# Written order for operand sums and early output splits, and one more step in two streams of a hybrid decoder layer

## The chip, the cores and the metric

One core of a Trainium2 chip runs the whole layer. The metric is the time of one execution on the device in microseconds, the median of three runs. TensorE (PE) multiplies matrices, and its weight loads are shown apart as PEld; VectorE (DVE) and ScalarE (ACT) do element-wise work; GpSimd (POOL) and SyncE (SP) mostly issue transfers here. PSUM is the memory that PE writes its sums to, in banks of 512 floats a partition.

## What is computed

For x of 2048 tokens by 1024 columns, in float32 throughout:

```python
h = _rmsnorm(x, norm1_w); proj = h @ w_in
o_hg = _hgrn2_mixer(...)   # 4 heads of 128: q, f, i, g; gated recurrence, then
#   o = o * lax.rsqrt(mean(o * o, axis=-1) + NORM_EPS) * norm_w * silu(g)
o_rw = _rwkv7_mixer(...)   # 8 heads of 64: S = S*w + (S a) b^T + v k^T, y = S r; group norm, gate
x = x + concat([o_hg, o_rw]) @ w_out
x = x + _conv_ffn(_rmsnorm(x, norm2_w), w_up, conv_w, conv_b, w_down)   # 1024 -> 5632 -> 2816 -> 1024
return _rmsnorm(x, final_norm_w)
```

## The kernel before

**Dense products.** Every large product keeps float32 accuracy by three matmuls in a reduced format: each operand is split into a rounded high part and the rest (`split`, L250 to L256, and `split_to`, L246 to L248: a copy on ACT, then a subtraction on DVE), and `mm3` (L268 to L272) issues high x high, high x low and low x high. The FFN products use a scheme with sums of operand blocks; `four_sums` (L238 to L244) makes four such sums on DVE.

**Two stages.** Stage one (`phase1`) covers the projections, both recurrences and three of the four output projections; stage two the last output projection and the FFN. Stage one walks over 4 blocks of 512 tokens. Three Python generators write its work down in turns:

- `dense`: jobs of 24 dense matmuls for 128 columns of the input projection (tile `pj`, two PSUM banks by turns, evacuated to `hf`, `hv`, `sgm`, `rkv` and others by `act` at L122 and by DVE), and in between the output projections (`out_block`), transposes (`turn`) and some set-up for stage two.
- `rw_stream`: eight calls of `rw_super`, two per block, each four RWKV heads: preparation, a small triangular solve on DVE (L793 to L814), the solve's matmuls (L821, L834, L847), copies of their result by ACT into `UV` and `M`, then state products (L867, L881, L895) and the state recurrence (L905 to L912).
- `hg_stream`: sixteen calls of `hg_unit`, one HGRN head each; at its end the output sums (L1064, L1065), their square, the split of the square (`osq` to `part`), two matmuls with a matrix of ones (L1083, L1084) for the mean square, Ln and Exp on ACT, and two products on DVE.

The driver takes one step (up to the next `yield`) of `rw_stream`, one of `hg_stream`, and then dense work worth 2000 ns by its own estimate (`TICK`).

**Set-up inside stage one.** `sum_load` (L459) loads four 128 x 1024 pieces of the normalised activations `h2d` into one row tile `xt`; `sum_make` calls `four_sums` on them and stores the results to `Ts`; both run twice (m = 0, 1), in the last block. `o_take` (L474) loads, four times, a piece of the mixer output of block 2 as `oraw` and splits it into `ohl`, which takes the place of the row tile; `out_block(2)` uses it as its first operand.

**What sets the order.** The kernel is written for a tile framework. [...] `tc.keep_in_program_order(i)` forbids the scheduler to put instruction i ahead of the one that was written just before it on the same engine. Functions of ACT come in tables; `act` (L111) ties an activation to the load of its table in written order, and a load is inserted where the next function in written order is in another table.

Of the kernel before, what the change touches and what calls it, by code (L numbers as in the profile page):

```python
# [67 lines left out]
def tile_layer(ctx, tc, consts, x, norm1_w, w_in, hg_lb_logits, hg_norm_w, rw_shift_mu, rw_w0, rw_w2,  # L68
# [4 lines left out]
    V, S, TE = nc.vector, nc.scalar, nc.tensor  # L73
# [40 lines left out]
    def act(out_, in_, func, **kw):  # L114

        want = tables.get(func)
        if want is not None and want != tab["now"]:
            pre = S.preload_act_table_set(want)
            for u_ in tab["uses"]:
                tc.add_manual_dep(pre.ins, u_.ins.name, NOSYNC, reason="table order")  # L120
            tab.update(now=want, pre=pre, uses=[])
        i_ = S.activation(out_, in_, func, **kw)  # L122
        if want is not None:
            tc.add_manual_dep(i_.ins, tab["pre"].ins.name, NOSYNC, reason="table order")
            tab["uses"].append(i_)
        return i_
# [13 lines left out]
    with tc.tile_pool(name="vp", bufs=1, reuse_waits="tile") as vp, tc.tile_pool(name="ps0", bufs=1, space=PSUM, reuse_waits="tile") as pools["ps"]:  # L140
        rows = vp.tile([P, P], F32, name="rows")
# [95 lines left out]

    def four_sums(b11, b12, b21, b22):  # L238

        V.tensor_sub(b11, b12, b11)  # L240
        V.tensor_sub(b12, b22, b12)
        V.tensor_sub(b22, b22, b11)
        V.tensor_sub(b21, b21, b22)
        return b11, b22, b12, b21  # L244

    def split_to(hi, lo, src):  # L246
        c_ = S.copy(hi, src)
        return c_, V.tensor_sub(lo, src, hi.bitcast(F32))  # L248
# [25 lines left out]
    def phase1(c1):  # L274
# [22 lines left out]
        def bank(kind):  # L297
            return ps.tile([P, 512], F32, tag=kind, name=kind, bufs=2)
# [119 lines left out]
        rows = {}  # L418
# [49 lines left out]
        def sum_make(m):  # L468
            def f():
                for i, t_ in enumerate(four_sums(*rows.pop(("S", m)))):  # L470
                    dma(tdst(0, i, 2 * m, 2), t_)
            return f

        def o_take(m):  # L474

            def f():
                if m == 0:
                    t_ = xp_.tile([P, 2, 2, 4, 256], F32R, tag="xt", name="ohl", bufs=1)
                    rows["O"] = [[t_[:, c, i] for i in range(2)] for c in range(2)]
                t_ = wp.tile([P, 2, 256], F32, tag="wraw", name="oraw", bufs=4)  # L480
                dma(t_, oT[2][2 * m * P:2 * (m + 1) * P, 0:256].rearrange("(k p) t -> p k t", p=P))
                ks = slice(2 * (m % 2), 2 * (m % 2) + 2)
                split_to(rows["O"][0][m // 2][:, ks, :], rows["O"][1][m // 2][:, ks, :], t_)
            return f

        def to_h(k, tp, w):
# [160 lines left out]
        def rw_super(nb, s_):  # L647
# [6 lines left out]
            def tile_(tag, shape, name):  # L654
                return rp.tile([P] + shape, F32, tag=tag, name=name)

            def bank2():
                return ps.tile([P, 2, BLK], F32, tag="rw", name="rw", bufs=2)

            def parts(src):  # L660
                hi, lo = (rp.tile([P, 2, BLK], F32R, tag=tag, name="part") for tag in ("XH", "E"))
                split_to(hi, lo, src)
                return hi, lo
# [134 lines left out]
            for j in range(31):  # L798
# [6 lines left out]
                if j % 4 == 3:  # L805
                    yield
            TZ = tile_("XH", [16, 16, 2], "TZ")
            V.transpose(TZ.rearrange("p c m f -> p (c m f)"), Ti.rearrange("m t c -> m c t"))
# [47 lines left out]
            for e in range(2):  # L856
                r0, c0 = er0(e), col0(1, e)
                act(M[r0:r0 + 64, 0, 1, :, :, 0:64], quv[1][c0:c0 + 64, :, :, 0:64], AF.Copy)
            yield
            XH = tile_("XH", [2, 9, 64], "XH")  # L860
            V.tensor_copy(XH[:, :, 0, :], Xc[:, 2 * s_:2 * s_ + 2, :])
            xp = bank2()
# [36 lines left out]
            for ch in range(8):  # L899
                b, e = ch // 2, ch % 2  # L900
                cs_ = slice(ch * 64, ch * 64 + 64)
                for u in U:
                    for h in range(2):
                        hr = slice(h * 64, h * 64 + 64)
                        TE.matmul(xp[hr, u, cs_], M[hr, 1, u, b, e, 0:64], XH[hr, u, ch, :], start=False,  # L905
                                  stop=ch == 7, tile_position=(h * 64, h * 64), skip_group_check=True)
                for u in U:
                    for h in range(2):
                        hr, c0 = slice(h * 64, h * 64 + 64), (h ^ u) * 64
                        TE.matmul(yp[c0:c0 + 64, u, cs_], XH[hr, u, ch, :], RT[hr, u, ch, :], start=False,  # L910
                                  stop=ch == 7, tile_position=(h * 64, c0), skip_group_check=True)
                V.tensor_mul(XH[:, :, ch + 1, :], xp[:, :, cs_], WC2[:, :, ch].broadcast_to([P, 2, 64]))  # L912
                yield
# [30 lines left out]
        def hg_unit(nb, j):  # L944
# [122 lines left out]
            act(sq, op, AF.Square)  # L1067
            hi, lo = (rp.tile([P, BLK], F32R, tag=tag, name="part") for tag in ("Sf", "VT"))
            split_to(hi, lo, sq)
            yield  # L1070
            ms = bank("hg")
            add_up(ms, ones, hi, lo)
# [13 lines left out]
        def rw_stream():  # L1086
            for n in range(2 * NBLK):
                while ready["rw"] <= n:
                    yield None
                yield from rw_super(n // 2, n % 2)  # L1090

        def hg_stream():
            for n in range(4 * NBLK):
                while ready["hg"] <= n:
                    yield None
                yield from hg_unit(n // 4, n % 4)
# [47 lines left out]
    with ExitStack() as c2:  # L1144
# [36 lines left out]
        with tc.tile_pool(name="op", bufs=1, reuse_waits="tile") as op_:  # L1181
# [61 lines left out]
            for dh in range(2):  # L1243
                accs = [pst("wacc") for _ in range(4)]
                for n, k in enumerate((0, 1, 4, 5, 2, 3, 6, 7)):
# [22 lines left out]
                    for q in range(12):  # L1268
                        i, t_ = (q % 4, q // 4) if first else (q // 3, q % 3)
# [355 lines left out]
```

## Time and profile before

| | us |
|---|---|
| median of 3 runs | 2640.78 (2636.36 to 2642.07) |
| the profiled execution | 2641.65, its span 2639.9 |
| PE busy in the span | 2551.4 (97%) |
| DVE busy, ACT busy | 1963.1 (74%), 1371.3 (52%) |
| granted PE clock, mean | 0.995 |
| stage one ends at about | 1302 |

A group's row reads: line, engine, operation, output<-input, shapes, count | busy time, mean ns of one | idle time of the engine just before, and what ended most of it. A wait's row reads: waiter <- what ended the wait: total us, times, longest. A row of a stretch reads: from:to, length, then busy time and count of PE, PEld, DVE, ACT and POOL, the granted clock, the DMA share and GB/s. A timeline row reads: start, duration, engine, line, operation, operands, count, and in brackets the idle time before it and what ended that. Busy PE spans overlap: a dense matmul is shown with 0.39 us, but the next starts 0.23 us after it.

### The profile page before, as it was taken

The numbers are of one execution on the slowest core, as the hardware profiler recorded it, in microseconds if no ns is written. First come the engines' busy times: TensorE is split into PE (matmuls) and PEld (weight loads), VectorE is DVE, ScalarE is ACT, GpSimd is POOL, SyncE is SP. The second block draws the span as 40 slices with busy tenths as digits, with TensorE's granted clock in tenths as the row PEclk, the third lists the DMA queues.
The fourth block names the chain that finished last, engine by engine and source line by source line (L and its number), as shares of the span: only waits on it lengthen the run. The fifth ranks groups of instructions, "written<-read, shape, count | busy, mean of one in ns | idle before, by whom it ended". The sixth has DMA issues, their size and how long they took to land.

```text
span 2639.9 us, 51054 instructions
## 1 busy us (share of the span) xinstructions
PE 2551.4 (97%) x19467; PEld 2046.3 (78%) x19467; DVE 1963.1 (74%) x3744; ACT 1371.3 (52%) x2258; POOL 381.4 (14%) x686
## 2 busy tenths in 40 slices
PE   7999999989999999999899999999999999999998
PEld 6877777767777767777678888877888888888887
DVE  4878676685666765777687799987998887766556
ACT  5565443555545555345466754456454544545444
POOL 6433222212222122222100000000000000000000
PEclk9999999999999999999999999999999999999999
DMA  8846463646645566845674477746763553998655
GB/s 305 240 153 193 157 176 110 149 149 216 193 168 145 158 211 187 277 145 149 204 253 134 130 235 255 235 158 217 239 207 129 174 169 132 332 321 283 200 190 187
DMA packets 380298, 518.98 MB, mean 197 GB/s; under 512 B 114463, under 2 KB 211093, under 8 KB 380053
## 3 DMA queue, kind: packets, MB, share of 16 engines
q1 hardware_dynamic: 325521, 337.38, 40.2%
q0 software_dynamic: 54464, 178.32, 21.0%
q8 instruction: 153, 2.51, 0.4%
q14 instruction: 92, 0.75, 0.1%
q10 hardware_dynamic: 68, 0.02, 0.0%
HBM read 372.99 MB, written 134.22 MB: 192 GB/s over the span
## 4 chain that ended last, share of the span: by engine, by line
PE 69%; DVE 13%; ACT 7%; DMA 7%; issue 4%; POOL 0%; SPq 0%; DVEq 0%; ACTq 0%; POOLq 0%
PE pj L270 7%; PE pj L271 7%; PE pj L272 7%; PE ua L270 4%; PE ua L272 4%; PE ua L271 4%; PE da L270 3%; PE da L271 3%; PE da L272 3%; PE ud L271 2%; PE ud L270 2%; PE ud L272 2%; PE db L272 2%; PE db L271 2%; PE db L270 2%
## 5 line engine op out<-in xcount | busy, mean ns | idle before, releaser
L270 PE MATMUL pj<-hh,wh 128*128 128x512 f32 x960 | 392.2, 409 | 4.5 <-ACT rkv L122 2.5
L271 PE MATMUL pj<-hl,wh 128*128 128x512 f32 x960 | 378.4, 394 | 0.0
L272 PE MATMUL pj<-hh,wl 128*128 128x512 f32 x960 | 378.3, 394 | 0.0
L270 PE MATMUL ua<-Bh,uwh 128*128 128x512 f32 x704 | 276.8, 393 | 3.0 <-ACT m L122 2.5
L272 PE MATMUL ua<-Bh,uwl 128*128 128x512 f32 x704 | 274.5, 390 | 0.0
L271 PE MATMUL ua<-Bl,uwh 128*128 128x512 f32 x704 | 274.2, 389 | 0.0
L270 PEld LDWEIGHTS pj<-hh,wh 128*128 128x128 f32 x960 | 181.2, 189 | 53.5 <-issue 8.3
L272 PEld LDWEIGHTS pj<-hh,wl 128*128 128x128 f32 x960 | 181.3, 189 | 39.5 <-issue 0.2
L271 PEld LDWEIGHTS pj<-hl,wh 128*128 128x128 f32 x960 | 181.3, 189 | 35.3 <-issue 0.6
L254 ACT CAST uwh<-uraw 128x512 fp32r<-128x512 f32 x220 | 134.2, 617 | 131.0 <-PE ua L271 54.0
L255 DVE TENSOR_TENSOR dal<-draw,dah 128x512 fp32r<-128x512 f32 x138 | 95.2, 690 | 110.9 <-ACT dah L254 108.5
L255 DVE TENSOR_TENSOR uwl<-uraw,uwh 128x512 fp32r<-128x512 f32 x220 | 147.1, 684 | 32.8 <-ACT uwh L254 32.7
L254 ACT CAST dah<-draw 128x512 fp32r<-128x512 f32 x138 | 85.8, 622 | 164.2 <-PE da L271 77.8
L270 PEld LDWEIGHTS ua<-Bh,uwh 128*128 128x128 f32 x704 | 132.3, 188 | 34.8 <-ACT m L122 7.0
L272 PEld LDWEIGHTS ua<-Bh,uwl 128*128 128x128 f32 x704 | 132.3, 188 | 28.1 <-DVE uwl L255 0.4
L271 PEld LDWEIGHTS ua<-Bl,uwh 128*128 128x128 f32 x704 | 132.2, 188 | 26.6
L1495 POOL DMA_DIRECT2D gd<-y x2 | 1.1, 540 | 949.0 <-DVE y L1493 949.0
L270 PE MATMUL ud<-Bh,uwh 128*128 128x512 f32 x352 | 138.0, 392 | 0.0
L272 PE MATMUL ud<-Bh,uwl 128*128 128x512 f32 x352 | 137.1, 390 | 0.0
L271 PE MATMUL ud<-Bl,uwh 128*128 128x512 f32 x352 | 137.0, 389 | 0.0
L271 PE MATMUL da<-dbl,dah 128*128 128x512 f32 x332 | 129.5, 390 | 0.2 <-DVE dbl L255 0.2
L272 PE MATMUL da<-dbh,dal 128*128 128x512 f32 x332 | 129.2, 389 | 0.0
(582 smaller groups left out, 6202.6 us busy)
## 6 DMA issues: line engine op xcount, KB each, us to landing
uraw<-in_w_up_dram SPq DMA_DIRECT2D x176, 256.0 KB, 3.2
woraw<-in_w_out_dram POOLq DMA_DIRECT2D x96, 256.0 KB, 3.6
br<-gd SPq DMA_DIRECT2D x88, 256.0 KB, 4.3
draw<-Sg SPq DMA_DIRECT2D x88, 256.0 KB, 3.0
draw<-Tw SPq DMA_DIRECT2D x88, 256.0 KB, 3.2
gd<-y SPq DMA_DIRECT2D x86, 256.0 KB, 3.0
Sg<-br SPq DMA_DIRECT2D x72, 256.0 KB, 2.5
xt<-x1d SPq DMA_DIRECT2D x32, 512.0 KB, 6.2
```

What stands on the lines that cost most here:

```text
L254: S.copy(hi, src)
L255: V.tensor_sub(lo, src, hi.bitcast(F32))
L270: TE.matmul(acc, lh, rh, start=first, stop=False, skip_group_check=skip)
L271: TE.matmul(acc, lh, rl, start=False, stop=False, skip_group_check=skip)
L272: TE.matmul(acc, ll, rh, start=False, stop=last, skip_group_check=skip)
L1495: (dma if end is None else nc.gpsimd.dma_start)(gd_[2 * h + b][fb * P:(fb + 1) * P, :], ys[0][:, b * BLK:(b + 1) * BLK])
```

## The change

The first of the four operand sums, and both halves of each early output split, are tied to the instruction written before them on their engine. `rw_super` gives up its turn once more between the copies of the solve's result and the state products, and `hg_unit` once more between the split of the square and the matmuls with ones. What is computed stays the same.

```diff
@@ four_sums
-        V.tensor_sub(b11, b12, b11)
+        tc.keep_in_program_order(V.tensor_sub(b11, b12, b11))
         V.tensor_sub(b12, b22, b12)
@@ o_take
-                split_to(rows["O"][0][m // 2][:, ks, :], rows["O"][1][m // 2][:, ks, :], t_)
+                for i_ in split_to(rows["O"][0][m // 2][:, ks, :], rows["O"][1][m // 2][:, ks, :], t_):
+                    tc.keep_in_program_order(i_)
             return f
@@ rw_super
                 act(M[r0:r0 + 64, 0, 1, :, :, 0:64], quv[1][c0:c0 + 64, :, :, 0:64], AF.Copy)
             yield
+            yield
             XH = tile_("XH", [2, 9, 64], "XH")
@@ hg_unit
             split_to(hi, lo, sq)
             yield
+            yield
             ms = bank("hg")
```

Since the scheduler places everything again, nearly all of stage one from the first HGRN unit's end on is in another order. Three places, without row numbers; line numbers of the changed kernel are 1 to 3 higher.

*ACT, seventh RWKV super, the copies of the solve's result* (`TTs`: solve; `UV`, `M`: the copies that the state products read; `osq`: HGRN's Ln and Exp). Before:

```order
L122 ACTIVATE TTs<-rw 32x8x32 x3
L118 ACT_TABLE_LOAD
L122 ACTIVATE osq<-hg,eps_71 128x512
L122 ACTIVATE osq<-osq 128x512
L122 ACTIVATE UV<-rw 64x4x128 x4
L122 ACTIVATE M<-rw 128x8x64
L122 ACTIVATE M<-rw 64x8x64 x2
L122 ACTIVATE VT<-hg 128x512
L122 ACTIVATE rkv_13175<-pj,omu 128x512
L247 CAST ohl<-oraw 128x512 x4
```

Now:

```order
L122 ACTIVATE TTs<-rw 32x8x32 x4
L118 ACT_TABLE_LOAD
L122 ACTIVATE UV<-rw 64x4x128 x4
L122 ACTIVATE M<-rw 128x8x64
L122 ACTIVATE M<-rw 64x8x64 x2
L122 ACTIVATE osq<-hg,eps_71 128x512
L122 ACTIVATE rkv_13106<-pj,omu 128x512
L122 ACTIVATE osq<-osq 128x512
L122 ACTIVATE Sf<-hf 128x256
L122 ACTIVATE VT<-hg 128x512
```

HGRN's Ln and Exp stood ahead of the copies and now stand behind them; the early output splits (`ohl`) no longer follow here.

*DVE, the second group of operand sums* (L240 to L243 on `xt`; L884 and L887, in the new text L886 and L889, finish the state products of one half super). Before:

```order
L241 TENSOR_TENSOR xt<-xt 128x1024
L974 TENSOR_TENSOR hf<-hf 128x128x2
L313 SCALAR_TENSOR_TENSOR rkv_13175<-pj,vt,rkv_13175 128x511
L314 SCALAR_TENSOR_TENSOR rkv_13175<-lastc,vt,rkv_13175 128x1
L965 TENSOR_TENSOR hX<-hq,hf 128x64x4
L315 COPY lastc<-pj 128x1
L971 TENSOR_TENSOR hX<-hk,Sf 128x64x4
L242 TENSOR_TENSOR xt<-xt 128x1024
L884 TENSOR_TENSOR M<-rw,cst 128x2x4x64
L887 TENSOR_TENSOR AR<-rw,AR 128x2x4x64
L972 TENSOR_TENSOR Sf<-Sf,hf 128x64x4
L243 TENSOR_TENSOR xt<-xt 128x1024
```

Now:

```order
L976 TENSOR_TENSOR hf<-hf 128x256
L973 TENSOR_TENSOR hX<-hk,Sf 128x128x2
L967 TENSOR_TENSOR hX<-hq,hf 128x128x2
L974 TENSOR_TENSOR Sf<-Sf,hf 128x128x2
L976 TENSOR_TENSOR hf<-hf 128x128x2
L973 TENSOR_TENSOR hX<-hk,Sf 128x64x4
L886 TENSOR_TENSOR M<-rw,cst 128x2x4x64
L889 TENSOR_TENSOR AR<-rw,AR 128x2x4x64
L967 TENSOR_TENSOR hX<-hq,hf 128x64x4
```

The sums are gone from between these rows. The first group now stands as one block a few rows ahead, the second some 65 rows behind it, after the end of the super's state recurrence (the copy to `Xc`).

*ACT, the first steps of the eighth super* (`ai`: sigmoids; `W`, `mk`: Exp and Ln; `sgm`, `hf`: sigmoids of projection columns). Before:

```order
L122 ACTIVATE ai<-rw,vt 128x512 x2
L122 ACTIVATE mk<-ai,oka,vt 128x512
L122 ACTIVATE ai<-rw,vt 128x512 x2
L122 ACTIVATE mk<-ai,oka,vt 128x512
L122 ACTIVATE sgm<-pj 128x512
L118 ACT_TABLE_LOAD
L122 ACTIVATE W<-mk 128x16x64
L122 ACTIVATE ai<-mk 128x1024
L122 ACTIVATE mk<-mk 128x1024
L247 CAST part<-BV 128x1024
L122 ACTIVATE mk<-mk 128x1024
L118 ACT_TABLE_LOAD
```

Now:

```order
L122 ACTIVATE osq<-osq 128x512
L118 ACT_TABLE_LOAD
L122 ACTIVATE sgm<-pj 128x512
L118 ACT_TABLE_LOAD
L122 ACTIVATE W<-mk 128x16x64
L122 ACTIVATE ai<-mk 128x1024
L122 ACTIVATE mk<-mk 128x1024
L247 CAST part<-BV 128x1024
L122 ACTIVATE mk<-mk 128x1024
L118 ACT_TABLE_LOAD
L122 ACTIVATE hf<-pj 128x512
L247 CAST ohl<-oraw 128x512
```

HGRN's Exp (`osq`) now falls between the sigmoids, with a table load on both sides of `sgm`, and the first early split follows `hf`. Over the whole program ACT has 53 table loads before and 65 now.

## The prediction

> **What bounds the kernel now.** I read the page, then busy time by stage, then TensorE's (PE's) waits, then the timeline around the longest of them.
>
> ```profile
> span 2639.9 us, 51054 instructions
> PE 2551.4 (97%) x19467; PEld 2046.3 (78%) x19467; DVE 1963.1 (74%) x3744; ACT 1371.3 (52%) x2258; POOL 381.4 (14%) x686
> ...
> 30.00:1302.00 1272.00, 1217.44 (x13603) 953.36 (x13602) 891.72 (x2111) 645.49 (x1078) 347.24 (x622) 0.99 0.59 181
> 1302.00:2640.00 1338.00, 1318.73 (x5807) 1081.91 (x5805) 1057.21 (x1598) 708.30 (x1145) 15.81 (x29) 1.00 0.64 210
> ```
>
> PE bounds both stages, so no removed work on another engine pays by itself; only PE's idle time does. The first stage, where every edit lies, has 1272 - 1217.4 = 54.6 us of it, the second 1338 - 1318.7 = 19.3. DVE (VectorE) and ACT (ScalarE) matter where PE waits for them:
>
> ```profile
> engine line waited for: us in total, times, longest us
> ...
> PE pj L270 <- ACT hh L247: 6.8, 6, 1.8
> PE hg L1084 <- DVE part L248: 5.3, 8, 1.8
> PE rw L881 <- DVE AR L887: 4.2, 1, 4.2
> ...
> PE rw L867 <- ACT M L122: 4.1, 7, 2.1
> PE pj L443 <- ACT hf L122: 4.1, 2, 2.1
> ...
> PE hg L1083 <- ACT part L247: 0.4, 2, 0.2
> ```
>
> Three rows belong to places that the change touches: L1084 is the norm sum right behind HGRN's split, L867 the first of RWKV's state products, and L881 one single wait whose cause the timeline shows:
>
> ```profile
> 1098.79 1.23 DVE L240 TENSOR_TENSOR xt<-xt 128x1024 f32<-128x1024 f32 x1 [2.45 <-DMA xt<-h2d]
> ...
> 1102.70 1.23 DVE L241 TENSOR_TENSOR xt<-xt 128x1024 f32<-128x1024 f32 x1
> ...
> 1105.70 1.22 DVE L242 TENSOR_TENSOR xt<-xt 128x1024 f32<-128x1024 f32 x1
> 1106.83 0.69 DVE L884 TENSOR_TENSOR M<-rw,cst 128x512 f32<-128x512 f32 x1
> 1107.43 0.68 DVE L887 TENSOR_TENSOR AR<-rw,AR 128x512 f32<-128x512 f32 x1
> ...
> 1108.26 0.69 PE L881 MATMUL rw<-M 64*64 64x64 f32 x32 [4.17 <-DVE AR L887]
> ...
> 1112.53 2.18 ACT L247 CAST ohl<-oraw 128x512 fp32r<-128x512 f32 x4 [11.45 <-DMA Ts<-xt]
> ```
>
> DVE stood 2.45 us at the second operand sum, whose load had not landed, then put three sums (3.7 us) ahead of L884 and L887; PE stood 4.17 us. ACT stood 11.45 us at the early output splits until the sums' stores had landed, but no PE wait ends on it there. After the three longest touched waits the granted clock is halved:
>
> ```profile
> 413.46 0.64 DVE L248 TENSOR_TENSOR part<-osq,part 128x512 fp32r<-128x512 f32 x1
> 414.15 0.50 PE L1084 MATMUL hg<-part,ones 128*128 128x512 f32 x1 [1.84 <-DVE part L248]
> ...
> 761.07 3.63 PE L867 MATMUL rw<-UV,KBT 128*64 128x64 f32 x58 [2.06 <-ACT M L122]
> ...
> 416.30:419.60 3.30, 3.30 (x9) 2.31 (x7) 0.88 (x3) 3.18 (x7) 0.19 (x1) 0.50 0.52 164
> 761.00:764.40 3.40, 3.30 (x55) 3.14 (x57) 3.23 (x9) 1.80 (x4) 0.00 (x0) 0.50 0.02 5
> 1109.20:1112.50 3.30, 3.30 (x23) 2.30 (x14) 1.92 (x4) 0.00 (x0) 1.07 (x2) 0.50 0.45 166
> ```
>
> Each stretch of about 3.3 us at 0.50 loses some 1.7 us more.
>
> **The change part by part.** No arithmetic and no DMA is added or removed; the edits give two streams one more step and pin some instructions. What counts is how far PE's own work now separates a producer from its consumer. A dense matmul takes 0.23 us from start to start:
>
> ```profile
> 408.00 0.39 PE L271 MATMUL pj<-hl,wh 128*128 128x512 f32 x1
> 408.23 0.39 PE L272 MATMUL pj<-hh,wl 128*128 128x512 f32 x1
> 408.46 0.40 PE L270 MATMUL pj<-hh,wh 128*128 128x512 f32 x1
> ```
>
> *HGRN's extra step.* Counted in the program, the dense matmuls between a unit's last output matmul (L1065) and its second norm matmul (L1084) go from a mean of 10.4 to 17.6 over the 16 units; two units gain none (13 to 11, 10 to 10). That is 7.2 x 0.23 = 1.7 us more cover, about the longest wait (1.8). Of 5.3 + 0.4 = 5.7 us I take 5.0; bounds 2.6 and 5.7.
>
> *RWKV's extra step.* Between the last matmul of the solve (L847) and the first L867 the eight supers have 11, 12, 12, 9, 10, 6, 10, 12 dense matmuls before and 17, 17, 18, 12, 18, 6, 18, 18 after: 1.4 us more in six, 0.7 in one, nothing in the sixth. Besides, ACT's norm logarithm and exponential now stand behind the copies that L867 waits for. Of L867's 4.1 us I take 3.5; bounds 0 and 4.1. Behind L867 on PE's queue wait only matmuls that need the same copies or are dense, so the step delays nobody beyond the stream itself.
>
> *Operand sums.* In the new order the second group's sums come some 65 rows after the first's, behind the whole state recurrence, so the load has landed, and nothing of it is left ahead of L884/L887. The first group is now one block of four (4 x 1.22 = 4.9 us) behind which the evacuation of one projection bank waits; the other bank covers that, since a job of 24 dense matmuls lasts 24 x 0.23 = 5.5 us. If it did not, PE would lose the 4.9. I take a gain of 4.0 (bounds -0.7 and 4.2).
>
> The early splits move behind the next super's sigmoids:
>
> ```profile
> L270 PEld LDWEIGHTS pj<-wh,ohl x32: 186/188/192, 1216.0 to 1258.3; 128*128 128x128 f32 x32
> ...
> woraw<-in_w_out_dram POOLq DMA_DIRECT2D x96, 256.0 KB, 3.6
> ```
>
> Their first use comes 100 us after they ran (1216.0 against 1112.5), so PE loses nothing. What queues with them: on SP the second sums' four stores stand ahead of the next super's key copies, which are made later anyway; on POOL the first four w_out loads, each waiting for a split to free its raw tile, stand among projection weight loads, and their casts two rows behind the last split on ACT. If a load came late, ACT would stand up to its 3.6 us, and PE less; I take 0, since two of the four tiles are free several evacuations earlier.
>
> *Clock.* The three halved stretches go with their waits: 3 x 1.7 = 5.1 (bounds 1.7 and 5.1). [...]
>
> *What is added: table loads.* The new order has 65 ACT table loads where the old has 53, all 12 in the first stage, because HGRN's Ln/Exp now falls between sigmoids.
>
> ```profile
> L118 ACT ACT_TABLE_LOAD  x53: 1283/1283/1283, 0.7 to 2252.5; - x53
> ...
> 488.27 2.13 ACT L122 ACTIVATE mk<-mk 128x1024 f32<-128x1024 f32 x2
> 490.43 1.28 ACT L118 ACT_TABLE_LOAD   x1
> 491.72 0.60 ACT L122 ACTIVATE hf<-pj 128x512 f32<-128x512 f32 x1
> ```
>
> 12 x 1.283 = 15.4 us of ACT. ACT is 645/1272 = 51% busy in this stage, so most is hidden; but a load ahead of a projection's evacuation is not: the "hf" above is one of the two waits of L443 (4.1 us). Bounds 0 and 15.4. Some 44 loads of this stage now show 4.1 us at PE, 0.1 each, which makes 1.2 for 12; they come in clusters (four ahead of one "hf"), so I take 3. [...]
>
> *The end of the stage.* RWKV's last super ends one step later against the dense work.
>
> ```profile
> 1291.17 0.39 PE L1084 MATMUL rw<-part,group 128*128 128x512 f32 x1
> ...
> 1301.48 1.22 DVE L938 TENSOR_TENSOR yo<-rw,yo 128x1024 f32<-128x1024 f32 x1
> ...
> 1302.62 1.28 DVE L413 TENSOR_TENSOR xh<-pj,xh 128x512 f32<-128x512 f32 x2
> ...
> 1304.55 1.20 PE L1270 MATMUL wacc<-wol,Bh 128*128 128x512 f32 x4 [0.50 <-DVE wol L248]
> ```
>
> Behind that L1084 PE had 33 dense matmuls left, now 24: 9 x 0.23 = 2.1 us less for the DVE chain (1291.2 to 1303.9), behind which wol waits. [...] I take 3, bounds 0 and 6.
>
> **Sum.** -5.0 - 3.5 - 4.0 - 5.1 + 3 + 3 = -11.6, against the profiled execution's own 2641.65: 2630. That execution is 0.9 above the median of 2640.78, which I leave inside the range.
>
> **Rivals.** *The other waits grow back.* All of stage one is re-ordered; touched waits are some 14 of its 54.6 us idle, and the other 40 are drawn anew (6.8 for hh, 4.1 for hf). For it: waits of 0.5 to 2 us are spread over all helpers. If they grow by a quarter (10 us), 2640: no change. Chance 0.21. *Table loads decide* (slower). At five places the new ACT order has Ln/Exp, load, sigmoid, load within a few rows, before the evacuations of two projection jobs. It decides once ACT's backlog exceeds one job's 5.5 us; then three exposed loads (3.8 us) and a half-clock stretch (1.7) cost 5.5 a place, 27.5 in all: 2641.65 - 17.6 + 3 + 27.5 = 2655. Against it: ACT is half idle, and the two present hf waits are only 2.1 each. Chance 0.11. *More than forecast*: no cost of loads, and both L443 waits go too, since at one of them "hf" now stands ahead of the Exp/Ln pair: 2641.65 - 17.6 - 4.1 = 2620. Chance 0.10. *The pins do nothing*: excluded for the order, but if the L881 wait reappears elsewhere on DVE, 4.0 + 1.7 is lost: 2636; inside the forecast's case.
>
> **How the numbers follow.** The forecast has 0.58 (own range 2622 to 2636). With bounds and rivals the range is 2615 (all gains, hf's waits too, no costs) to 2645 (half of the small gains, both costs). A measurement here tells 0.2%, 5.3 us: faster 0.58 + 0.10 = 0.68, same 0.21, slower 0.11.
>
> **What would show it.** Right: L1084's and L867's rows in PE's waits under 1 us each, no 4 us wait at L881, no stretch at 0.50 near 416, 761 and 1109, DVE's L240 with no wait for its load. Wrong: ACT rows ("hf", "sgm", "hh") at the top of PE's waits with more than 20 us together, halved stretches behind table loads, or a wait of wacc over 5 us.

## The result, and the profile after

The changed kernel takes 2649.98 us (median of 9 runs, 2646.02 to 2655.68), the kernel before on the same chip 2642.04 (9 runs, 2634.74 to 2647.19). The ratio is 1.0029, with a 95% interval of 1.0019 to 1.0039: slower by some 7.7 us, where 11.6 us less were forecast. The profiled execution took 2646.02 us.

The page, and then the two stages as windows (from:to, length, busy PE, PEld, DVE, ACT and POOL with counts, granted clock, DMA share, GB/s):

```profile
span 2644.2 us, 51061 instructions
PE 2549.3 (96%) x19467; PEld 2051.0 (78%) x19467; DVE 1967.8 (74%) x3744; ACT 1388.6 (53%) x2270; POOL 381.7 (14%) x686
```

```profile
30.00:1308.00 1278.00, 1215.86 (x13601) 954.71 (x13599) 896.31 (x2111) 661.45 (x1090) 346.14 (x621) 0.99 0.58 180
1308.00:2644.00 1336.00, 1317.45 (x5802) 1084.34 (x5802) 1056.29 (x1597) 708.85 (x1143) 16.18 (x30) 0.99 0.64 211
```

ACT has 12 instructions and 17 us more, 15.4 of them the 12 table loads. PE's idle time in stage one is 1278 - 1215.86 = 62.1 us, 7.5 more than before. Its waits:

```profile
engine line waited for: us in total, times, longest us
...
PE pj L270 <- ACT hh L247: 7.0, 6, 3.1
PE rw L822 <- DVE TZ L809: 6.0, 6, 2.3
PE pj L443 <- ACT hf L122: 4.5, 1, 4.5
PE pj L443 <- ACT xt L122: 3.8, 4, 1.7
PE rw L883 <- DVE AR L889: 3.7, 3, 1.9
PE wacc L1273 <- DVE Bl L248: 3.3, 1, 3.3
...
PE wacc L1273 <- ACT Bh L247: 2.1, 1, 2.1
...
PE hg L1087 <- DVE part L248: 0.9, 1, 0.9
...
PE rw L869 <- ACT M L122: 0.3, 1, 0.3
```

The waits that the change touches went as forecast: HGRN's norm sums (now L1087) from 5.7 us to 0.9, the state products (L869) from 4.1 to 0.3, the one wait of 4.17 us for AR is gone, though AR is now waited for three times, 3.7 us together (longest 1.9). What came instead stands above them. "hf" and "xt" at L443 are the transposes between two projections (5.0 us before, 8.3 now); TZ is the solve's result (2.9 before); "wacc" is the first work after stage one, with Bl (2.1 before) and Bh (none before).

The granted clock changed places too. Three stretches at half clock that are new or longer than before, and then the three that the prediction named:

```profile
213.20:223.40 10.20, 7.13 (x29) 6.03 (x30) 8.94 (x12) 9.59 (x15) 1.08 (x2) 0.50 0.04 16
288.30:295.10 6.80, 6.80 (x78) 4.26 (x77) 6.71 (x20) 5.04 (x11) 3.19 (x6) 0.50 0.63 173
1308.90:1319.10 10.20, 6.37 (x14) 4.30 (x14) 5.48 (x10) 3.36 (x7) 1.30 (x3) 0.50 0.85 290
416.00:419.40 3.40, 3.40 (x72) 2.39 (x72) 3.09 (x15) 1.55 (x3) 0.68 (x2) 1.00 0.57 188
761.00:764.40 3.40, 3.40 (x47) 2.51 (x50) 0.26 (x2) 3.11 (x6) 1.06 (x2) 1.00 0.39 145
1109.00:1112.40 3.40, 3.40 (x71) 2.69 (x61) 3.26 (x11) 0.60 (x1) 1.08 (x3) 1.00 0.47 122
```

The old three are at 1.00. Two more new ones, not shown, are 6.83 us long at 582 and 3.41 us at 838. Up to 1320 us the half clock lasted 20.5 us in all before (3.41 four times, 6.83 once) and 44.4 now; at half speed 24 us more cost about 12 (an estimate).

**Where the table loads bite.** ACT's timeline around 210 us, before and then with the change, and the PE rows that wait on it with the change:

```profile
205.71 1.28 ACT L118 ACT_TABLE_LOAD   x1
...
211.59 1.28 ACT L118 ACT_TABLE_LOAD   x1
```

```profile
205.69 0.63 ACT L122 ACTIVATE osq<-osq 128x512 f32<-128x512 f32 x1
206.34 1.28 ACT L118 ACT_TABLE_LOAD   x1
207.63 0.60 ACT L122 ACTIVATE sgm<-pj 128x512 f32<-128x512 f32 x1
...
208.95 1.28 ACT L118 ACT_TABLE_LOAD   x1
...
212.26 1.28 ACT L118 ACT_TABLE_LOAD   x1
213.56 0.60 ACT L122 ACTIVATE hf<-pj 128x512 f32<-128x512 f32 x1
214.17 1.28 ACT L118 ACT_TABLE_LOAD   x1
```

```profile
214.21 1.11 PE L443 MATMUL pj<-ident,xt 128*128 128x128 f32 x4 [4.54 <-ACT hf L122]
217.06 1.11 PE L443 MATMUL pj<-ident,xt 128*128 128x128 f32 x4 [1.74 <-ACT xt L122]
```

Four loads in 8 us, three of them ahead of the sigmoid "hf": between HGRN's Exp ("osq"), a sigmoid ("sgm"), RWKV's Exp and "hf"; before there were two. The evacuation "hf" comes late by them, PE stands 4.54 us (1.98 at this place before), and the clock is halved for 10.2 us.

**At the end of the stage**, PE, and then DVE before and with the change:

```profile
1307.93 1.31 PE L1273 MATMUL wacc<-woh,Bh 128*128 128x512 f32 x4 [2.14 <-ACT Bh L247]
1309.73 2.07 PE L1273 MATMUL wacc<-wol,Bh 128*128 128x512 f32 x4 [0.49 <-DVE wol L248]
1315.14 2.07 PE L1273 MATMUL wacc<-woh,Bl 128*128 128x512 f32 x4 [3.34 <-DVE Bl L248]
```

```profile
1298.16 0.68 DVE L1077 TENSOR_TENSOR hgg<-osq,hgg 128x512 f32<-128x512 f32 x1
```

```profile
1307.20 0.68 DVE L1080 TENSOR_TENSOR hgg<-osq,hgg 128x512 f32<-128x512 f32 x1
...
1314.40 0.69 DVE L248 TENSOR_TENSOR Bl<-uraw,Bh 128x512 fp32r<-128x512 f32 x1 [4.72 <-DMA oT<-hgg]
```

"hgg" is the product of the last HGRN unit, 9 us later than before. The split that makes Bl stands until a transfer that the trace names as its store (oT<-hgg) has landed, 7 us behind the product, and PE stands with it.

### The profile page after: what moved, and what is told of

Read it like the earlier page. It is cut to its first block, busy times and chain, and to the rows that moved or that the text cites. A ratio compares the mean times of both kernels' runs of the same rounds, so it can differ in the third digit from the quotient of the medians.

```text
span 2644.2 us, 51061 instructions
## 1 busy us (share of the span) xinstructions
PE 2549.3 (96%) x19467; PEld 2051.0 (78%) x19467; DVE 1967.8 (74%) x3744; ACT 1388.6 (53%) x2270; POOL 381.7 (14%) x686
## 4 chain that ended last, share of the span: by engine, by line
PE 50%; issue 10%; DVE 6%; DMA 5%; ACT 3%; POOL 2%; SPq 0%; POOLq 0%; DVEq 0%; ACTq 0%
PE ua L270 5%; PE ua L272 5%; PE ua L271 5%; PE da L271 3%; PE da L270 3%; PE da L272 3%; PE pj L270 3%; PE ud L272 2%; PE ud L271 2%; PE ud L270 2%; PE pj L271 2%; PE pj L272 2%; PE db L270 2%; PE db L272 2%; PE db L271 2%
```

## The experiments

Two theories are told in the expectations. A: the added table loads and the later end of the stage cost what the vanished waits gave. B: any new order costs by itself, since waits that nobody aimed at are drawn anew. All ratios are to the kernel before, run beside each.

**The parts alone and in pairs.** The "pins" are the edits of `four_sums` and `o_take`; the steps are the `yield` of HGRN (10 added table loads) and that of RWKV (6; both together 12). For the pins:

```diff
-        V.tensor_sub(b11, b12, b11)
+        tc.keep_in_program_order(V.tensor_sub(b11, b12, b11))
...
-                split_to(rows["O"][0][m // 2][:, ks, :], rows["O"][1][m // 2][:, ks, :], t_)
+                for i_ in split_to(rows["O"][0][m // 2][:, ks, :], rows["O"][1][m // 2][:, ks, :], t_):
+                    tc.keep_in_program_order(i_)
```

> Only the pins on the operand sums and the early output splits; no extra step in either stream; 53 table loads as before. If added table loads and the later end of stage one make the loss (theory A), this kernel has neither and keeps the gain at L881: some 4 us of wait and one half-clock stretch (1.7) less than before, ratio 0.998. If any new order costs as much by itself (theory B, the untouched waits are drawn anew), it is as likely slower as faster, within 8 us either way.

HGRN's step alone, and RWKV's step alone (in `hg_unit` and `rw_super`, one line each):

```diff
             split_to(hi, lo, sq)
             yield
+            yield
```

> Only HGRN's extra step; 63 table loads. Theory A: the norm waits go (5 us, and the half-clock stretch near 416), ten more loads cost PE waits of 4 to 7 us at the first steps of the second super (near 214 us) with a half-clock stretch behind, and the end of the stage is later: 2 to 8 us slower than before, ratio 1.001 to 1.003. Theory B: no preference for the stretch near 214.

```diff
             yield
+            yield
             XH = tile_("XH", [2, 9, 64], "XH")
```

> Only RWKV's extra step; 59 table loads. Theory A: L867's waits go (4 us and the stretch near 761), six more loads cost about as much; the end of the stage is one step later (2 to 5 us): 0 to 5 us slower, ratio 1.000 to 1.002. Theory B: anything within 8 us, with new waits at places without added loads.

The pairs, each the change less one edit:

> The pins and HGRN's extra step, without RWKV's: 63 table loads. If the parts simply add (pins 0.9964, HGRN's step 1.0032) it is 0.9996. Theory A expects that within 0.001, since the pins change neither the loads nor the end. Theory B lets it lie up to 0.003 to either side.

> The pins and RWKV's extra step, without HGRN's: 59 table loads. If the parts add (0.9964, 1.0018) it is 0.9982; theory A expects that within 0.001, theory B lets it lie up to 0.003 to either side.

> Both extra steps without the pins: 65 table loads. If the parts add (1.0032, 1.0018) it is 1.0050, and with the pins' gain the change itself would be 1.0014, where it is 1.0029. Theory A expects less than the sum for the two steps, since together they add 12 loads and not 10 + 6, about 1.004. Theory B lets it lie up to 0.003 from 1.0050.

| pins | HGRN's step | RWKV's step | ratio (95%) |
|---|---|---|---|
| x | | | 0.9964 (0.9949 to 0.9979) |
| | x | | 1.0032 (1.0019 to 1.0045) |
| | | x | 1.0018 (1.0006 to 1.0030) |
| x | x | | 1.0011 (0.9998 to 1.0023) |
| x | | x | 0.9967 (0.9957 to 0.9977) |
| | x | x | 1.0057 (1.0037 to 1.0076) |
| x | x | x | 1.0029 (1.0019 to 1.0039) |

Averaged over what they are combined with, the pins give 0.0034 (9 us), HGRN's step costs 0.0045 (12 us) and RWKV's 0.0016 (4 us). Every part keeps its sign in each combination. In the three pairs the parts add up to within 0.0015, 0.0015 and 0.0007. That doesn't tell A from B: A had expected the pairs with the pins within 0.001 and both steps together below their sum (about 1.004), B allowed 0.003, and each interval is itself some 0.001 to 0.002 to either side. Nor did HGRN's step alone lose its time where A expected it, near 214 us: from 207 to 235 it lost 1.5 us. For the pins, the stretch around the old wait, in the kernel before and then with the pins alone:

```profile
1095.00:1130.00 35.00, 29.95 (x545) 23.33 (x547) 23.53 (x55) 9.50 (x16) 8.09 (x16) 0.95 0.69 236
```

```profile
1095.00:1130.00 35.00, 34.42 (x679) 27.30 (x680) 19.32 (x58) 7.51 (x16) 7.47 (x14) 1.00 0.59 200
```

PE is busy for 4.5 us more of these 35, at full clock: the wait and its halved stretch are gone.

**The steps without more table loads.** First, with the pins, each stream got its new step and gave up an earlier one:

```diff
@@ rw_super (ahead of the solve, L790), and hg_unit (L954)
-            yield
@@ both, at the places of the change
+            yield
```

> All of the change, but each stream gives up one earlier turn (HGRN's behind its first transposes, RWKV's behind the copies into RHS), so a unit and a super have as many steps as before; 53 table loads, and the added cover of the norm sum (mean 16 dense matmuls) and of the state products (mean 14) is mostly kept. Theory A: the waits of the norm sum and of L867 stay away, no wait near 214 beyond the old 2 us, and the end of the stage is less late: 10 to 17 us faster than before, ratio 0.994 to 0.996. Theory B: the order is again a new one, so the time is within 8 us of before, and not tied to the loads.

Measured: 1.0059 (1.0040 to 1.0077), 25 us more than the pins alone, with 53 loads. That is against both theories as they stood (A expected 10 to 17 us less than before, B within 8 us of it; it is 16 more), but a step given up moves as much as one added. Its waits of PE:

```profile
PE hg L990 <- issue: 7.5, 3, 2.6
...
PE rw L868 <- DMA xh<-in_x_dram: 3.3, 1, 3.3
```

Neither row is in the other traces with such sizes; the run shows that where a stream's steps stand matters by 1%, and doesn't tell A from B.

So the next two keep all steps and add new ones at single units, on top of the pins, all with 53 loads.

```diff
@@ hg_unit
+            if (nb, j) == (1, 0):
+                yield
@@ rw_super
+            if (nb, s_) == (2, 0):
+                yield
```

> The pins, and the extra steps only at the two places with the longest touched waits: HGRN's fifth unit (wait of 1.84 us at 414) and RWKV's fifth super (2.06 us at 761). 53 table loads, as before. Against the pins alone (ratio 0.9964): theory A expects the two waits and the two halved stretches behind them gone and nothing in return, 1.84 + 2.06 + 2 x 1.7 = 7.3 us less, a ratio of 0.9936. Theory B expects the same up to 414, the two waits gone, and new waits behind each place: anywhere from 0.991 to 1.000, with the losses in rows behind 420 that no edit touches.

```diff
@@ hg_unit
+            if (nb, j) == (1, 1):
+                yield
```

> The pins, and one extra step at one place where PE does not wait: HGRN's sixth unit (at 471, no wait of its norm matmuls). 53 table loads. Theory A expects the time of the pins alone, 0.9964, within 0.001. Theory B expects it up to 8 us away from that (0.9934 to 0.9994), to either side, with other waits in the rows behind 471 and the same ones ahead of it.

Measured: 0.9954 (0.9940 to 0.9968) for the two places and 0.9974 (0.9963 to 0.9985) for the idle one, 2.6 us below and 2.6 above the pins alone. Both are within a measurement of the pins: the gain of the two places over them has an interval from 3 us of loss to 8 of gain. Removing the two longest waits gave about a third of the 7.3 us that A expected, and a step where nothing waits costs no more than B's smallest sizes. The trace of the two places shows where the rest may have gone. The wait at 414 is 0.3 us there, the one at 760 is gone, but ACT puts a cast that waits for a load ahead of the copies of the solve's result, and PE has a new wait (0.5 us with the pins alone):

```profile
563.86 0.62 ACT L247 CAST hh<-oraw 128x512 fp32r<-128x512 f32 x1 [1.55 <-DMA oraw<-oT]
```

```profile
PE rw L848 <- ACT TTs L122: 2.7, 1, 2.7
```

No edit aims at that place; it is what B had said, in a small size. A stretch at half clock is left too, at 420 us instead of 416, though no wait of PE in the 5 us ahead of it is over 0.7 us.

```diff
@@ hg_unit
+            if 4 * nb + j in (4, 6, 7, 10, 14):
+                yield
@@ rw_super
+            if 2 * nb + s_ in (3, 4, 5, 6):
+                yield
```

> The pins and nine of the 24 extra steps, picked so that ACT keeps the 53 table loads of before and the last super and the last unit are as before: HGRN's units 5, 7, 8, 11 and 15 of 16, RWKV's supers 4 to 7 of 8. They hold the two longest touched waits (1.84 and 2.06 us), 1.0 us at the seventh super and 0.4 to 0.6 us at others: some 6 us of wait and two halved stretches (3.4 us). Against the pins alone (0.9964): theory A, in which added table loads and the later end are what costs, expects some 9 us less, a ratio of 0.993. Theory B, in which a new order draws the untouched waits anew and mostly worse, expects no gain over the pins or a loss, 0.996 to 1.000.

Measured: 0.9951 (0.9937 to 0.9966), 2628.56 us, below the kernel before and the change, and the lowest ratio of all kernels that compute the whole layer. Nine steps that add no load cost nothing on balance; they gain some 3.4 us over the pins, where A expected 9 and B none, and the two intervals overlap.

```profile
L118 ACT ACT_TABLE_LOAD x53 | 68.0, 1283 | 1.7 <-PEq L1615 0.7
```

**Table loads without the steps.**

```diff
+    def swap():
+        for want in ("natural_log_exp_and_others", "sigmoid_and_others"):
+            ...
@@ rw_super, behind the two sigmoids
+            swap()
```

> The kernel before with 13 table loads more on ACT (66, where the change has 65): once a super, behind its sigmoids, the table is changed to Ln/Exp and back. No step is added and nothing is pinned; the other instructions keep their written order. Theory A (the added table loads and the later end of stage one cost what the vanished waits gave, about 17 us together) expects 5 to 15 us more than before, a ratio of 1.002 to 1.006, with waits of PE on rows of ACT behind the added loads. Theory B (each new order draws the waits that nobody aimed at anew) expects under 3 us, a ratio of 1.001 or less, since the order stays.

Measured: 1.0080 (1.0062 to 1.0099), 21 us. The trace has more loads than the expectation says, 74 and not 66: `swap` made 16, and five more stand at L122, the line of the functions themselves:

```profile
L118 ACT ACT_TABLE_LOAD x53 | 68.0, 1283 | 1.7 <-PEq L1619 0.7
L131 ACT ACT_TABLE_LOAD x16 | 20.5, 1283 | 0.2
L122 ACT ACT_TABLE_LOAD x5 | 6.4, 1283 | 0.3 <-DVE tl L322 0.2
```

So 21 added loads cost 21 us, 1.0 each, if all of it is theirs: other instructions moved in this kernel as well. It loses where the change loses, by the same rows; around 495 us (ACT, then PE, whose L451 is L443 in the kernel before):

```profile
492.72 2.57 ACT L131 ACT_TABLE_LOAD   x2
...
502.32 1.28 ACT L118 ACT_TABLE_LOAD   x1
503.61 0.60 ACT L122 ACTIVATE hf<-pj 128x512 f32<-128x512 f32 x1
```

```profile
501.41 0.66 PE L451 MATMUL pj<-ident,xt 128*128 128x128 f32 x4 [2.33 <-ACT xt L122]
504.26 1.97 PE L451 MATMUL pj<-ident,xt 128*128 128x128 f32 x8 [2.20 <-ACT hf L122]
```

To see it by place, the dense matmuls of two traces can be matched by their number (all have the same 3456 in the same order), and the time between two of them compared. In us against the kernel before; places by its times; the added loads in brackets:

| place | pins | nine steps | HGRN's | RWKV's | change | loads only |
|---|---|---|---|---|---|---|
| 207 to 235 | -0.5 | -0.6 | 1.5 (2) | 2.5 (2) | 6.1 (4) | 1.9 (2) |
| 281 to 400 | -0.2 | -0.5 | 5.4 (2) | 3.4 (2) | 4.8 (2) | 5.6 (2) |
| 454 to 506 | 0.0 | -0.1 | 5.7 (2) | 0.9 (2) | 1.0 (2) | 3.2 (2) |
| 782 to 871 | 0.0 | 1.3 | 3.6 (2) | 1.3 | 4.5 (2) | 2.4 (2) |
| these four | -0.7 | 0.1 | 16.2 | 8.1 | 16.4 | 13.1 |
| 400 to 454 (L1084's wait) | -0.6 | -1.6 | -1.8 | -6.7 | -7.0 | -0.2 |
| 713 to 782 (L867's) | -1.2 | -3.9 | -2.2 | -3.9 | -3.6 | -1.3 |
| 1073 to 1163 (L881's) | -5.5 | -7.9 | -0.1 | 2.1 | -4.7 | 1.4 |
| last dense matmul to the FFN's first | -2.7 | -4.0 | -3.2 | 2.7 | 4.4 | -2.5 |

The change gains 15.3 us at the three places it aims at, and loses 16.4 at four where loads were added. The kernels with 53 loads lose little there: the two in the table nothing, those with a step at two places or an idle one 0.9 and 1.9, and the one that gave up earlier steps 5.7.

Three things limit what the table can carry. Each column is one execution. The change, the same without its last steps and the steps without the pins have one and the same order on ACT and DVE up to 1089 us; between these three the rows at 207 and 782 agree (6.1, 6.1, 6.2 and 4.5 three times), but the row at 454 is 1.0, 1.1 and 3.6, and the row at 281 is 4.8, 5.1 and 1.1. That last row follows the time that the load of the next block's x takes to land (5.4, 5.8 and 4.4 us in these three, 3.9 before) and not the table loads: a kernel with 27 loads, below, loses 7.4 us there, with 5.1 us to land. So 11.6 of the 16.4 us are left for the loads. And one stretch without any added load is not in the table: from 506 to 713 us the change loses 7 to 8 us, these two relatives of it 3 to 6, and the nine steps 7.9, where the pins lose 1.5. Some of the loss belongs to the new order itself.

**The last step.**

```diff
@@ rw_super
-            yield
+            if (nb, s_) != (NBLK - 1, 1):
+                yield
@@ hg_unit
-            yield
+            if (nb, j) != (NBLK - 1, 3):
+                yield
```

> The change without the two extra steps of the last RWKV super and the last HGRN unit, so that the last super ends at the same step against the dense work as before. 65 table loads. My term for the end of the stage was 3 us (bounds 0 and 6): if it is right, 3 us less than the change, a ratio of about 1.002 to before, and the waits of wacc near 1308 (2.3 and 3.7 us) under 1 us. If the end is not a matter of the last step, 1.003 as the change.

Measured: 0.9996 (0.9982 to 1.0010), 8.7 us less than the change. The windows behind the stage, of the change first:

```profile
1302.00:1355.00 53.00, 47.03 (x194) 37.49 (x193) 34.81 (x56) 27.92 (x47) 2.35 (x4) 0.90 0.78 264
```

```profile
1302.00:1350.00 48.00, 47.77 (x208) 38.47 (x209) 36.30 (x59) 26.78 (x47) 2.38 (x4) 1.00 0.86 296
```

Without the last steps PE is busy for all but 0.2 of 48 us, more matmuls in 5 us less; there is no wait of wacc and no halved stretch. From the last dense matmul to the FFN's first it takes 4.1 us less than before the change, with them 4.4 more: 8.5, nearly the whole difference. Neither step does this alone. With HGRN's step the stretch takes 3.2 us less than before (3.5 less with the pins), with RWKV's 2.7 more (1.2 more with the pins); only with both does HGRN's last product come behind the last dense matmul. Here, then, the parts don't add, by some 5 us.

**Steps without table functions.** All four kernels of this group leave out the norms' reciprocal roots and the gates, by functions on the same tiles that need no table:

```diff
-            act(sq, ms, AF.Ln, bias=eps6, scale=1.0 / 128)
-            act(sq, sq, AF.Exp, scale=-0.5)
+            act(sq, ms, AF.Identity, bias=eps6, scale=1.0 / 128)
+            act(sq, sq, AF.Identity, bias=half, scale=0.0)
@@ the same for RWKV's group norm; the sigmoids of the projections
-                act(sgm, acc, AF.Sigmoid)
+                act(sgm, acc, AF.Identity, scale=0.1)
...
-                act(t_, acc, AF.Sigmoid)
+                act(t_, acc, AF.Square, bias=half, scale=0.05)
```

> The kernel before with its table functions between the dense jobs replaced by functions that need no table (the Ln/Exp of HGRN's norm and of RWKV's group norm, and the sigmoids of the projection columns): the same ACT instructions on the same tiles, wrong values, since norms and gates are left out. 27 table loads. It is the base for the next three, which have 27 as well. Theory A (a table load among the projections costs PE about 1 us; 21 added ones cost 21) expects it some 15 to 25 us faster than the kernel before, 0.990 to 0.994. Theory B (the order costs, not the loads) expects 0.996 to 1.000.

> Both extra steps on that base, without the pins; 27 table loads, as the base. With the loads the two steps cost 15 us (1.0057). Theory A expects that the 12 loads were most of it: without them the steps remove some 12 us of waits and halved clock and pay some 7 at the end, so against the base of this group a ratio of 0.997 to 1.000. Theory B expects the cost to stay, 1.004 to 1.007 against the base.

> The whole change (pins and both steps) on that base; 27 table loads. With the loads it is 1.0029. Theory A expects 0.994 to 0.997 against the base of this group (the pins' 9 us, and the steps at no cost or a gain). Theory B expects 1.001 to 1.004.

> The whole change but for the extra step of the last RWKV super and the last HGRN unit, on that base; 27 table loads. With the loads this gave 0.9996 where the change gives 1.0029, some 9 us. If those 9 us are the end of the stage (DVE's chain behind the last group norm, with fewer dense matmuls ahead of it), it is 6 to 9 us faster than the whole change on this base too. If they were drawn by the loads, it is within 3 us of it.

| on 27 loads | to the kernel before | to the base | the same with the loads |
|---|---|---|---|
| base | 0.9985 (0.9969 to 1.0000) | 1 | 1 |
| both steps | 1.0001 (0.9988 to 1.0014) | 1.0016 (0.9996 to 1.0036) | 1.0057 |
| the change | 0.9967 (0.9952 to 0.9981) | 0.9982 (0.9961 to 1.0003) | 1.0029 |
| without the last steps | 0.9933 (0.9907 to 0.9958) | 0.9948 (0.9918 to 0.9978) | 0.9996 |

(The intervals to the base are combined from the two beside them.) Three things follow. Without the added loads the change is 0.0047, 12.4 us, cheaper (interval 6 to 18), and the steps 0.0041, 11 us: the loads are most of what the steps cost. The end of the stage costs 9.0 us here too (interval 1 to 17), so it isn't a matter of the loads. The rows of the change on this base show it again, PE and DVE:

```profile
1303.54 2.07 PE L1274 MATMUL wacc<-woh,Bl 128*128 128x512 f32 x4 [5.95 <-DVE Bl L249]
```

```profile
1302.79 0.69 DVE L249 TENSOR_TENSOR Bl<-uraw,Bh 128x512 fp32r<-128x512 f32 x1 [7.33 <-DMA oT<-hgg]
```

And theory A missed the base itself: 26 loads taken out gave 4 us (interval 0 to 8), 0.15 each, not 15 to 25; B had that one right. Both steps and the change on this base (1.0016 and 0.9982) fall between what A and B expected. By these figures the loads that were there cost little and the added ones 1.0 each. A weakness stays: the base was ordered anew as well, and loses 7.4 us between 281 and 400 that its kernels with steps don't lose, so part of the 12.4 may be that base's bad luck. Without those 7.4 us the added loads would cost 5, and those that were there 0.4 each. By places, in 207 to 235, 454 to 506 and 782 to 871 the change loses 6.5 on this base against 11.6 with the loads. Between some 5 and 12 us, with the measurement's own interval on top, the size stays open.

So A is borne out for the added loads, in sign, and for the end of the stage, on both bases. It had the loads that were there and the gain of the steps wrong, and small new waits such as B speaks of are there too (TTs at 565, TZ at 287, the stretch from 506 to 713).

## Why the prediction was wrong

The forecast was 2630 us with a range to 2645; the time is 2650. In the prediction's own terms, the right column from differences of runs (0.001 is 2.64 us):

| term | forecast | by the runs |
|---|---|---|
| operand sums and their halved stretch | -4.0 - 1.7 | -9.5 (the pins alone) |
| waits of both steps and two halved stretches | -5.0 - 3.5 - 3.4 | -4.2 (no last steps, 27 loads: -13.7, less the pins) |
| table loads | +3 | +12.4 (the change with its loads less without) |
| end of the stage | +3 | +9.0 (27 loads), +8.7 (65 loads) |
| sum | -11.6 | +7.7 |

The last column adds up by the way it is made; what bears it out are the second values of the end, the pins' gain in all four pairs, and the places. If the 7.4 us that the base with 27 loads loses between 281 and 400 are taken for luck, the second row is +3.2 and the third +5.0: together the two rows are 17 us off, and how the 17 divide stays open by 7.

All the signs of being right that the prediction named came true, and the time went the other way: they speak of the waits that were aimed at. Of its signs of being wrong one came (a halved stretch behind table loads); "hh" and "hf" have 11.5 us together, not 20, and the longest wait of wacc is 3.3 us, not 5.

- **What bounds the kernel, and the aimed waits: right.** L1084, L867 and L881 went to 0.9, 0.3 and no 4 us wait, three stretches went back to full clock, L240 no longer waits for its load. The early splits hold PE nowhere, as said.
- **Operand sums: right, undersized.** The pins alone give 9.5 us where 5.7 were summed; in their one trace 5.5 of it is at L881, and 2.7 behind the stage, which I had not seen.
- **The steps' gain: at most a third of the sum came.** The waits did go, 8.6 us of them, but with the two longest removed alone only some 2.6 us came back (interval -3 to 8), so the time hardly followed. I took the waits that nobody aimed at as unchanged; the rival "the other waits grow back" had said otherwise. New ones came: TTs at 565 us in the kernel with the two places, and in the change TZ, 2.31 us at 287 with a stretch of 6.83 us at half clock behind. The chain to TZ is one that no edit touches: the load of the next block's x is issued right behind the last reader of its buffer on DVE (at 272.14 us before, 275.35 now) and took 3.9 us to land before and 5.4 now (why it took longer stays open); ACT's norm stands behind it, "tl" behind that, DVE's solve behind "tl", and PE at TZ. Before, and then with the change, on ACT and on DVE:

```profile
276.06 1.06 ACT L122 ACTIVATE nsq<-xt 128x1024 bf16<-128x1024 f32 x1 [0.76 <-DMA xt<-in_x_dram]
...
277.81 0.75 DVE L313 SCALAR_TENSOR_TENSOR tl<-pj,vt,tl 128x511 f32<-128x511 f32 x1 [0.33 <-ACT tl L122]
```

```profile
280.80 1.06 ACT L122 ACTIVATE nsq<-xt 128x1024 bf16<-128x1024 f32 x1 [2.07 <-DMA xt<-in_x_dram]
...
282.56 0.75 DVE L313 SCALAR_TENSOR_TENSOR tl<-pj,vt,tl 128x511 f32<-128x511 f32 x1 [1.83 <-ACT tl L122]
```

- **Table loads: the step that failed most.** I divided the 4.1 us of L443's waits by the 44 loads that stood there (0.1 each), and took 3 us for 12. The mean price of those was about right: 26 of them taken out gave 0.15 each, 0.4 at most by the reckoning above. But an added load isn't an average one. It falls among the loads that are already ahead of "hf", where PE already waits, so that by these runs some 0.4 to 1.0 us of its 1.283 reaches PE, the halved clock behind it included. The rival "table loads decide" had this mechanism, with 5.5 us a place at five places and 2655; the three places of the table that are left for the loads lost 6.1, 1.0 and 4.5 us. Its chance of 0.11 was too small, and the argument against it (ACT is half idle in this stage) was an average over the stage where the queue at one place decides. The rows with the change still show 1.283 us for each of the 65 loads.
- **The end of the stage: right place, wrong chain, mis-sized.** I followed RWKV's last chain on DVE to wol, and priced 9 matmuls (2.1 us) and some halved clock, 3 us together; by the runs the end costs some 9. No run shows the halved clock in that term (0.9 of the 3 us) as something that a wait's length brings: in the trace before, the wait of 2.06 us at 761 had a halved stretch with it, and those of 2.09 us at 492, 2.52 at 987 and 2.14 at 1312 had none. For RWKV's step alone 3 would have been near (2.7 us in its trace), but I looked at one stream at a time. The wait for wol is 0.5 us. What is late is HGRN's last product, which now runs at 1307.2 where the last dense matmul ends at 1305.8; before, it ran at 1298.16, with 4.5 us of dense work behind it. Its store, and what waits for that, had been covered; uncovered, PE waits 2.14 us at Bh and 3.34 at Bl, with 10.2 us at half clock.
- **Clock: three stretches went, as said, and on balance 24 us more came.** Those at 213, 288 and 1309 stand at or behind new waits of 4.54, 2.31 and 2.14 us; the one at 838 follows a wait of 1.42, and the one at 582 no wait over 0.6 us in the 10 us ahead of it. The sum had a gain for each wait removed and nothing for waits added.

## What to carry to other kernels

Price an added operation by the place where it lands, not by the mean over those that are there: here the 26 loads taken out had cost some 0.15 us each (0.4 at most), those put into a cluster ahead of an evacuation 0.4 to 1.0. When a stream gets one more step, count what the step adds on every engine at every repetition, keep it to the repetitions where it adds nothing, and leave out the last one, behind which no other work covers the stores and reloads that follow. Look at the streams together there, since neither step did this harm alone. Here nine of 24 steps, with the pins, made 0.9951 of what all 24 made 1.0029; the pins without any step made 0.9964, and the difference between the first and the last is within a measurement.

## What the runs showed of the hardware

In the traces of both kernels the halved clock comes in stretches of 3.41, 6.83 and 10.24 us up to 1320 us. 10.2 us of it came with the wait of 4.54 us that ended at 214, and again behind the wait of 2.14 us that ended at 1308, with the one of 3.34 us inside the stretch, where PE issued only 14 matmuls in all. The stretch from 207 to 235, with the wait of 4.54 us, took 6.1 us longer than before, where one wait of 1.98 us had 3.41 us of half clock behind it. I had counted 3.3 us of it for each wait.

In these two traces, up to 1320 us, neither the length of one wait nor PE's share of busy time tells by itself where the clock was halved:

| trace | halved from | for | PE busy in the 3.41 us ahead | longest wait of PE that ended in the 10 us ahead |
|---|---|---|---|---|
| before | 214.87 | 3.41 | 34% | 1.98 |
| | 416.26 | 3.41 | 62% | 1.84 |
| | 761.00 | 3.41 | 42% | 2.06 (ended at 761.07) |
| | 1109.16 | 3.41 | 26% | 4.17 |
| | 1266.18 | 6.83 | 55% | 1.13 |
| the change | 213.18 | 10.24 | 0% | 4.54 (ended at 214.21) |
| | 288.27 | 6.83 | 49% | 2.31 |
| | 581.81 | 6.83 | 73% | 0.60 |
| | 837.81 | 3.41 | 42% | 1.42 |
| | 1267.89 | 6.83 | 36% | 1.03 (one of 3.09 ended inside, at 1270.28) |
| | 1308.85 | 10.24 | 37% | 2.14 (one of 3.34 ended inside, at 1315.14) |

A wait of 1.84 us that ended at 414 had a halved stretch behind it; waits of 2.09, 2.52 and 2.14 us that ended at 492, 987 and 1312 in the same trace had none. From 982.87 to 986.28 us before, and from 499.90 to 503.31 with the change, PE was busy for 48 and 50%, and the clock stayed at 1.00 there and behind; ahead of the stretch at 416.26 it was busy for 62%, and ahead of the one at 581.81 for 73%.
